# A pair's first product put into the bank of its sums by ScalarE and added to there by TensorE, in the feed-forward stage of an encoder block

## The chip, the cores and the metric

The kernel runs on one core of a Trainium2 chip, in one launch. The metric is the device time of one execution in microseconds. Of the kernel before, three runs were timed: 2977.9, 2979.1 and 2979.88 us, median 2979.1. One further execution was profiled. The engines are named as the profile names them: PE is TensorE (its matmuls), PEld its loads of weights, DVE is VectorE, ACT is ScalarE, POOL is GpSimd, SP is SyncE, which here issues the DMAs.

## The reference

One block of an encoder on 2048 tokens of width 1024: a mixing part (two groups of heads), a feed-forward part, and an embedding that is added through a gate. The change touches the feed-forward part alone:

```python
def conv_gated_mlp(xn, w_up, conv_w, conv_b, w_down):
    u = dwconv3_centred(xn @ w_up, conv_w, conv_b)
    gate, val = jnp.split(u, 2, axis=-1)
    return (jax.nn.silu(gate) * val) @ w_down
...
        h = h + conv_gated_mlp(rms_norm(h, ln_ffn_g[l]), w_up[l], conv_ffn_w[l],
                               conv_ffn_b[l], w_down[l])
```

`w_up` is 1024 x 5632, so gate and value have 2816 columns each; the convolution runs over three neighbouring tokens; `w_down` is 2816 x 1024.

## The kernel before, in words

**Products.** Everything is float32. A product is made as three products of split operands: a high part that TensorE takes fast (type fp32r) and a low part, the rest. `split` (L113) makes them: ScalarE casts the high part (L117), VectorE subtracts it from the source to get the low one (L120). `mm3` (L130 is its last line) issues low x high, high x low and high x high.

**Pairs.** `up_down` runs the two big products of the feed-forward part as a sequence of 68 pairs of 128-row tiles. Pairs 0 to 43 multiply by `w_up` (22 for the first half of the tokens, 22 for the second; each has one tile of gate and one of value columns), pairs 44 to 67 by `w_down` (three blocks of eight, each over a part of the 2816 rows). A pair is a 2 x 2 product of blocks, done in seven products in place of eight, after Strassen. The sums of the stationary operand (S1 to S4) and of the moving one (T1 to T4) are made ahead. Its seven products are A11 B11, S1 T1, S2 T2, A12 B21, S3 T3, A22 T4 and S4 B22. Each takes 12 matmuls of 128 x 512 (four depth steps of three), 9 in the last block.

**Banks.** A pair has two PSUM tiles of two banks: `fxy` with x and y, `fzs` with z and a spare bank, each tile in a ring of two. A11 B11 goes into x, and A12 B21 is added there. S1 T1 goes into z, and S4 B22 is added there. S2 T2 goes into y, and S3 T3 and A22 T4 are added there one after the other. Between two of them y is read out, since each partial sum is wanted by itself: after S2 and after S3 in the same pair, after A22 in the next. What all four results have in common, the first product A11 B11, is added outside: in the up pairs ScalarE copies x to a tile p1 (L1493), and VectorE adds p1 to y at each read; in the down pairs VectorE adds x into the output rows.

**After the products.** In up pairs the results lie in `ug` (gate) and `uv` (value), 1024 tokens and two of the neighbours each. `conv` (L1418) runs the three taps: an ACTIVATE on ScalarE, two scalar_tensor_tensor on VectorE for each of gate and value, Silu on ScalarE (L1434), a multiply, and a DMA to `hid_d`. In down pairs VectorE adds the results to rows of h (`fh`), which a DMA loaded, and another stores.

**Operands.** The moving operands of a block (seven names of four tiles) are loaded and split by `load_op` (L1280 is the DMA) when the block changes: at pairs 22, 44, 52 and 60. The loads of a name are issued where its old tiles have had their last use. `up_load` and `up_prep` fetch and split the stationary tiles of the pairs to come. `steps` spreads other sums over the pairs, `ple` the beginning of the last stage over the last block.

**Order.** The code is written pair by pair, but a scheduler puts the instructions of each engine in order; each engine then works strictly in its list, and semaphores hold it where an operand or a bank isn't ready. VectorE and ScalarE have one list each for reads of banks, splits of operands and the convolution, so a read of a bank can stand behind a split that waits for a DMA.

## Time and profile before

| what | value |
|---|---|
| timed runs | 2977.9, 2979.1, 2979.88 us |
| the profiled execution | 2982.03 us |
| its span | 2980.3 us |
| mean granted TensorE clock | 0.995 |
| TensorE matmul, busy | 2922.8 us, 98%, 14858 matmuls |
| VectorE, busy | 2065.7 us, 69% |
| ScalarE, busy | 1355.9 us, 45% |
| the stage `up_down` in the span | about 1436 to 2748 us |

Times in the views count from the start of the span. A row of the timeline has the start, the time taken, the engine, the line, the operation, output and inputs, and how many ran; in brackets is how long the engine stood idle before it and what released it. A row of waits has the engine that waited, the line waited for, the total, the number and the longest. Matmuls overlap each other (one lasts about 0.39 us, and the next starts 0.23 us after it), so a busy TensorE isn't yet one that goes at its full rate.

### The profile page before, as it was taken

To read this page: it belongs to the slowest core of one execution; us is meant where nothing else is said; L and a number is where in the kernel's file an instruction comes from. 1 tells how busy PE (TensorE), PEld (TensorE's weight loads), DVE (VectorE), ACT (ScalarE), POOL (GpSimd) and SP (SyncE) were. 2 spreads that over 40 slices of the span, in tenths; PEclk is the share of its full clock that TensorE was granted. 3 is DMA by queue.
4 is the path that set the end of the run, shared out by engine and by line. 5 is a ranking of instruction groups with operands and counts; after the bars stand their busy time and mean duration, and the time that the engine had idled before them with its cause. 6 is when DMAs were issued, how large, how long until landed. Compare 5 with 4: busy or idle time off the path is not lost. (4 is left out here: it accounts for less than half of the span.)

```text
span 2980.3 us, 40726 instructions
## 1 busy us (share of the span) xinstructions
PE 2922.8 (98%) x14858; PEld 2456.4 (82%) x14858; DVE 2065.7 (69%) x3799; ACT 1355.9 (45%) x2648; POOL 141.8 (5%) x262
## 2 busy tenths in 40 slices
PE   8999999999999999999999999999999999999999
PEld 7888888888889888788788887788887787877887
DVE  7522555677777777636688888778878777687665
ACT  6311544656656565523444445444445232233444
POOL 3100000000000000001000000000000000000111
PEclk9999999999999999999999999999999999999999
DMA  6512445343333343568544544557746656575221
GB/s 190 124 59 94 141 131 156 119 151 98 100 98 101 95 126 103 168 191 282 187 142 170 198 164 168 177 180 239 234 150 186 198 195 219 173 243 203 80 80 64
DMA packets 377401, 460.20 MB, mean 154 GB/s; under 512 B 30176, under 2 KB 263152, under 8 KB 377200
## 3 DMA queue, kind: packets, MB, share of 16 engines
q1 hardware_dynamic: 377200, 457.59, 47.9%
q8 instruction: 117, 1.92, 0.3%
q14 instruction: 84, 0.69, 0.1%
HBM read 294.26 MB, written 163.25 MB: 154 GB/s over the span
## 5 line engine op out<-in xcount | busy, mean ns | idle before, releaser
L130 PE MATMUL fxy<-op,fw 128*128 128x512 f32 x3168 | 757.9, 395 | 16.2 <-DVE fh L1387 11.6
L130 PEld LDWEIGHTS fxy<-op,fw 128*128 128x128 f32 x3168 | 590.4, 189 | 164.8 <-DVE fh L1387 21.9
L130 PE MATMUL fzs<-op,fw 128*128 128x512 f32 x1584 | 386.9, 390 | 1.1 <-DVE xt L1152 1.1
L130 PEld LDWEIGHTS fzs<-op,fw 128*128 128x128 f32 x1584 | 297.6, 188 | 63.5 <-DVE xt L1152 1.3
L130 PE MATMUL bk<-wsp,xh 128*128 128x512 f32 (+1 forms) x768 | 233.9, 386 | 0.0
L117 ACT CAST pt<-tb 128x512 fp32r<-128x512 f32 x256 | 147.1, 587 | 176.1 <-PE tb L977 175.5
L919 DVE TENSOR_REDUCE mx<-bk 128x1 f32<-128x512 f32 x256 | 175.2, 685 | 68.2 <-PE bk L918 63.7
L130 PE MATMUL ppv<-pt,kv 128*128 128x256 f32 x1536 | 203.9, 287 | 0.0
L120 DVE TENSOR_TENSOR pt<-tb,pt 128x512 fp32r<-128x512 f32 x256 | 174.2, 685 | 37.7 <-ACT pt L117 36.4
L130 PE MATMUL fxy<-op,fwd 128*128 128x512 f32 x792 | 192.0, 391 | 2.9 <-DVE c L1387 1.4
L937 ACT ACTIVATE pe<-bk,nm 128x512 f32<-128x512 f32 x256 | 174.6, 696 | 32.5 <-DVE nm L931 27.1
L130 PEld LDWEIGHTS ppv<-pt,kv 128*128 128x128 f32 x1536 | 189.0, 191 | 0.5 <-ACT pt L117 0.4
L130 PE MATMUL bk<-wo,yhl 128*128 128x512 f32 x744 | 176.1, 395 | 3.6 <-DVE yhl L120 3.6
L130 PE MATMUL pgp<-pw,x3s 128*128 128x512 f32 (+1 forms) x792 | 178.6, 384 | 0.0
L130 PEld LDWEIGHTS fxy<-op,fwd 128*128 128x128 f32 x792 | 147.8, 188 | 36.5 <-DVE uv L1387 3.3
L130 PEld LDWEIGHTS pgp<-pw,x3s 128*128 128x128 f32 x792 | 144.5, 188 | 28.3
L1387 DVE TENSOR_TENSOR fh<-fh,fxy 128x512 f32<-128x512 f32 (+1 forms) x139 | 104.9, 768 | 89.0 <-PE fxy L130 87.6
L130 PEld LDWEIGHTS bk<-wo,yhl 128*128 128x128 f32 x744 | 139.2, 189 | 32.5 <-DVE yhl L120 4.1
L130 PEld LDWEIGHTS bk<-wsp,xh 128*128 128x128 f32 x768 | 145.1, 189 | 25.0
L130 PE MATMUL bk<-wsp,xl 128*128 128x512 f32 (+1 forms) x384 | 150.5, 392 | 8.2 <-DVE xl L120 8.2
L117 ACT CAST fw<-hraw 128x1024 fp32r<-128x1024 f32 (+1 forms) x72 | 70.4, 980 | 191.8 <-PE fxy L130 116.1
L130 PE MATMUL bk<-xh,wqk 128*128 128x512 f32 x480 | 157.5, 393 | 0.0
(332 smaller groups left out, 5024.3 us busy)
## 6 DMA issues: line engine op xcount, KB each, us to landing
fwr<-in_w_up SPq DMA_DIRECT2D x66, 512.0 KB, 4.0
fh<-h_d SPq DMA_DIRECT2D x48, 512.0 KB, 5.0
h_d<-fh SPq DMA_DIRECT2D x48, 512.0 KB, 2.8
s_d<-fwr SPq DMA_DIRECT2D x44, 512.0 KB, 3.2
fws<-s_d SPq DMA_DIRECT2D x44, 512.0 KB, 3.6
rw<-row_d SPq DMA_DIRECT2D x32, 512.0 KB, 5.1
hraw<-hid_d SPq DMA_DIRECT2D x30, 512.0 KB, 4.5
tsum<-in_w_down SPq DMA_DIRECT2D x44, 256.0 KB, 4.2
```

The costliest lines, as they stand in the source:

```text
L117: nc.scalar.copy(hi, src)
L120: (sub or nc.vector).tensor_tensor(lo, src, _f(hi), op=ALU.subtract)
L130: mm = lambda *a, **k: self.nc.tensor.matmul(*a, **k, skip_group_check=more)
L919: nc.vector.tensor_reduce(s.mx[:, kb:kb + 1], ps, axis=AX.X, op=ALU.max)
L937: nc.scalar.activation(s.pe[:, kb % 2], s.banks[kb], AF.Exp, bias=s.nm, scale=ASCALE, accum_out=s.rs[:, kb:kb + 1])
L1387: add = lambda o, a, b: tt(o, a, b, op=ALU.add)
```

## The change

From pair 2 on (`seeded`), ScalarE copies the first product from bank x into bank y as soon as it is complete. S2, S3 and A22 are then all added to what is in the bank by TensorE (`more=True`, so that none of their matmuls starts the bank anew), and each read of y already holds the first product. With that

- VectorE's additions of p1 to y go: in up pairs the reads of y after S2 and after A22 become copies on ScalarE, and the read after S3 stays an addition on VectorE, but of z's first product (S1 T1, which ScalarE copies to a tile p5 when it is complete) in place of p1; the second addition to uv goes. In down pairs the addition of x to half a row and that of 128 x 1024 to a whole row go.
- `rest` is split: `rest_y` (A22, added to the previous pair's y) comes after S1 as before, `rest_z` (S4, added to the previous pair's z) after A12 of the pair. `conv` is split into its halves, the value's after `rest_y`, the gate's after `rest_z`.
- B22 of a new block is loaded after `rest_z`, and no longer together with T4 before S2. The steps of other sums move from after the rest to after the reads of S2 and of S3.
- within a product the twelve matmuls run as high x high for the four depth steps, then low x high, then high x low.

The number of matmuls stays. The diff without its repeats (`twice` and the old `rest`, `conv` and `prod` are in the listing above):

```diff
@@ prod
-            for k, (xh, xl) in enumerate(ops):
-                ks = slice(k * P, (k + 1) * P)
-                self.mm3(out, wh[:, ks], wl[:, ks], xh, xl, not more and k == 0, k == len(ops) - 1, more)
+            first, last = not more, len(ops) - 1
+            for a, lo in ((wh, 0), (wl, 0), (wh, 1)):
+                for k, parts in enumerate(ops):
+                    nc.tensor.matmul(out, a[:, k * P:(k + 1) * P], parts[lo], start=first,
+                                     stop=lo == 1 and k == last, skip_group_check=more)
+                    first = False
@@ rest, now rest_y and rest_z
+            elif s.seeded:
+                nc.scalar.copy(s.uv[:, 2:2 + SB], s.y)
             else:
                 add(s.uv[:, 2:2 + SB], s.p1, s.y)
+
+        def rest_z(s):
+
             prod(s.z, s.ops["S4"], "B22", True)
@@ the loop over pairs
+            s.seeded = i > 1
             prod(x, s.ops["A11"], "B11")
-            if i < NUP + 2:
-                s.p1 = s.spare if i > NUP else self.at(f"t{6 + i % 2}", [P, SB], name="p1")
+            if s.seeded:
+                nc.scalar.copy(s.y, x)
+            else:
+                s.p1 = self.at(f"t{6 + i}", [P, SB], name="p1")
                 nc.scalar.copy(s.p1, x)
             if s.down:
                 s.o = outs.pop(i)
-                p1 = s.p1 if i < NUP + 2 else x
-                add(s.o[0][:, H], s.o[0][:, H], p1)
-            if i > NUP:
-                add(twice(s.o[1]), twice(s.o[1]), p1.unsqueeze(1).broadcast_to([P, 2, SB]))
...
             prod(s.z, s.ops["S1"], "T1")
+            if s.seeded and not s.down:
+                s.p5 = self.at(f"t{6 + i % 2}", [P, SB], name="p5")
+                nc.scalar.copy(s.p5, s.z)
...
             if prev:
-                rest(prev)
-                if prev.i in steps:
-                    self.p1tag = f"t{6 + prev.i % 2}"
-                    next(steps[prev.i])
+                rest_y(prev)
+                if not prev.down:
+                    conv(prev, 1)
             if j == 0 and blk:
                 load(blk, "T4")
-                load(blk, "B22")
             side(2, 3, 4, 6)
-            prod(s.y, s.ops["S2"], "T2")
+            prod(s.y, s.ops["S2"], "T2", s.seeded)
             if s.down:
                 add(s.o[0][:, H], s.o[0][:, H], s.y)
             else:
                 s.ug = self.at(f"u{i % 2}", [P, 2 * SB + 2], name="ug")
-                add(s.ug[:, 2 + SB:2 + 2 * SB], s.p1, s.y)
+                if s.seeded:
+                    nc.scalar.copy(s.ug[:, 2 + SB:2 + 2 * SB], s.y)
+                else:
+                    add(s.ug[:, 2 + SB:2 + 2 * SB], s.p1, s.y)
+            if i in steps:
+                next(steps[i])
...
             side(7)
-            if prev and not prev.down:
-                conv(prev)
+            if prev:
+                rest_z(prev)
+                if not prev.down:
+                    conv(prev, 0)
+            if j == 0 and blk:
+                load(blk, "B22")
...
             prod(s.y, s.ops["S3"], "T3", True)
             if i == NUP:
                 c22 = self.at("t7", [P, SB], name="c22")
-                add(c22, s.p1, s.y)
+                nc.scalar.copy(c22, s.y)
                 add(c22, c22, s.z)
                 s.o += self.down_out(NUP, (1,))
-                add(s.o[1][:, L], s.o[1][:, L], s.p1)
...
             else:
                 s.uv = self.at("u2", [P, 2 * SB + 2], name="uv")
-                add(s.uv[:, 2 + SB:2 + 2 * SB], s.p1, s.y)
-                add(s.uv[:, 2 + SB:2 + 2 * SB], s.uv[:, 2 + SB:2 + 2 * SB], s.z)
+                add(s.uv[:, 2 + SB:2 + 2 * SB], s.p5 if s.seeded else s.p1, s.y)
+                if not s.seeded:
+                    add(s.uv[:, 2 + SB:2 + 2 * SB], s.uv[:, 2 + SB:2 + 2 * SB], s.z)
```

How that moves the instructions. The first place is TensorE in an up pair of the first half. Of the names, `fw` are split stationary tiles (A11 and A12 of a pair are the two halves of one, so they share a name; `op` are the moving operands), `fwd` is A22. Before, from the last matmuls of S2 (15246, 15247) through a part of the next pair's A11 (15366, 15367) to A12 (15231, 15232):

```order
L130 MATMUL fxy<-op,fw_15246 128x512 x2
L130 MATMUL fxy<-op,fw_15247 128x512
L130 MATMUL fxy<-op,fw_15246 128x512 x2
L130 MATMUL fxy<-op,fw_15367 128x512
L130 MATMUL fxy<-op,fw_15366 128x512 x2
L130 MATMUL fxy<-op,fw_15367 128x512
L130 MATMUL fxy<-op,fw_15366 128x512
L130 MATMUL fxy<-op,fw_15232 128x512
L130 MATMUL fxy<-op,fw_15231 128x512 x2
L130 MATMUL fxy<-op,fw_15232 128x512
L130 MATMUL fxy<-op,fw_15231 128x512 x2
```

After, one pair from S1 (15234) through A22 of the previous pair (`fwd`), S2 (15240, 15241), the first four of S4 of the previous pair (15106), A12 (15225, 15226), the other eight of S4, to S3 (15234):

```order
L1401 MATMUL fzs<-op,fw_15234 128x512 x12
L1401 MATMUL fxy<-op,fwd 128x512 x12
L1401 MATMUL fxy<-op,fw_15240 128x512 x4
L1401 MATMUL fxy<-op,fw_15241 128x512 x4
L1401 MATMUL fxy<-op,fw_15240 128x512 x4
L1401 MATMUL fzs<-op,fw_15106 128x512 x4
L1401 MATMUL fxy<-op,fw_15225 128x512 x4
L1401 MATMUL fxy<-op,fw_15226 128x512 x4
L1401 MATMUL fxy<-op,fw_15225 128x512 x4
L1401 MATMUL fzs<-op,fw_15106 128x512 x8
L1401 MATMUL fxy<-op,fw_15234 128x512 x12
```

Between S2 and A12, which both use the tile `fxy`, five matmuls of the next A11 stood before, and four of S4 stand now; between A12 and S3 stand eight of S4.

The second place is VectorE at the switch to the second block of down pairs (pair 52). `fh` are rows of h, and L1387 adds to them; `op` are the split operands. Before:

```order
L1387 TENSOR_TENSOR fh<-fh,fxy 128x512
L1387 TENSOR_TENSOR fh<-fh,fxy 128x1024
L1387 TENSOR_TENSOR fh<-fh,fxy 128x512
L120 TENSOR_TENSOR op<-opr,op 128x512 x2
L1387 TENSOR_TENSOR fh<-fh,fzs 128x512
L120 TENSOR_TENSOR op<-opr,op 128x512 x6
L1387 TENSOR_TENSOR fh<-fh,fxy 128x512
L120 TENSOR_TENSOR fw_22352<-hraw,fw_22351 128x1024
L120 TENSOR_TENSOR fwd<-hraw,fwd 128x512
```

After:

```order
L120 TENSOR_TENSOR op<-opr,op 128x512 x4
L1387 TENSOR_TENSOR fh<-fh,fxy 128x512
L120 TENSOR_TENSOR fwd<-hraw,fwd 128x512
L1368 TENSOR_TENSOR hraw<-hraw 128x512
L1369 TENSOR_TENSOR hraw<-hraw 128x512
L1375 TENSOR_TENSOR hraw<-hraw 128x512
L1376 TENSOR_TENSOR hraw<-hraw 128x512
L1387 TENSOR_TENSOR fh<-fh,fxy 128x512
L1387 TENSOR_TENSOR fh<-fh,fzs 128x512
L120 TENSOR_TENSOR fw_22322<-hraw,fw_22322 128x1024
L120 TENSOR_TENSOR fw_22317<-hraw,fw_22316 128x1024
L120 TENSOR_TENSOR op<-opr,op 128x512 x4
```

Of the last eight subtractions of the block's operands (T4 and B22), all stood ahead of the addition of S2's bank before (the seventh row, behind the runs of two and of six). After, a run of four stands ahead of it (the addition is the second row), and the other four stand behind the additions that follow.

The third place is ScalarE in a steady up pair of the second half, after the change. L1502 is the copy into the bank, L1442 Silu, L1515 the copy of z to p5, L1412 and L1533 the new reads of y, L1434 the ACTIVATE, L1553 the copy of A12's bank:

```order
L1502 COPY fxy<-fxy 128x512
L1442 ACTIVATE fgv<-fgv 128x1024
L1515 COPY p_19677<-fzs 128x512
L1412 COPY uv<-fxy 128x512
L117 CAST fwd<-fwr 128x512
L1434 ACTIVATE fgv<-uv,fcw 128x1024
L1533 COPY ug<-fxy 128x512
L117 CAST fw_19730<-fws 128x1024
L1553 COPY ug<-fxy 128x512
```

Between the read of y after A22 (L1412) and that after S2 (L1533) stand a cast of `fwd` and the value's ACTIVATE; of these copies only that of A12's bank stood in ScalarE's list before, and the one of the first product to p1.

More of the change, by code (lines that the diff above doesn't have):

```diff
@@ L1388, in up_down @@
         L, H = slice(0, SB), slice(SB, 2 * SB)
-        twice = lambda t: t.rearrange("p (a t) -> p a t", a=2)
         NUP, blocks = self.NUP, self.BLOCKS
@@ L1398, in prod, with rest_y @@
             ops = self.xop[x]
-            for k, (xh, xl) in enumerate(ops):
-                ks = slice(k * P, (k + 1) * P)
-                self.mm3(out, wh[:, ks], wl[:, ks], xh, xl, not more and k == 0, k == len(ops) - 1, more)
-        def rest(s):
+            first, last = not more, len(ops) - 1
[4 more added lines that the diff above has]
+                    first = False
+        def rest_y(s):
             prod(s.y, s.ops["A22"], "T4", True)
@@ L1416, in rest, with conv @@
                 add(s.ug[:, 2 + SB:2 + 2 * SB], s.ug[:, 2 + SB:2 + 2 * SB], s.z)
-        def conv(s):
+        def conv(s, half):
             b, c = divmod(s.i, NC2)
-            ts = []
-            for half, u in enumerate((s.ug, s.uv)):
-                ct = half * NC2 + c
-                if b:
-                    nc.vector.tensor_copy(u[:, 0:2], edge[:, ct])
-                else:
-                    nc.vector.memset(u[:, 0:2], 0.0)
-                t = self.at(("w7", "w11")[half], [P, 2 * SB], name="fgv")
-                nc.scalar.activation(t, u[:, 0:2 * SB], AF.Identity, bias=taps[:, 3, ct:ct + 1], scale=taps[:, 0, ct:ct + 1])
-                for tap in (1, 2):
-                    nc.vector.scalar_tensor_tensor(t, u[:, tap:tap + 2 * SB], taps[:, tap, ct:ct + 1], t,
-                                                   op0=ALU.mult, op1=ALU.add)
-                nc.scalar.copy(edge[:, ct], u[:, 2 * SB:2 * SB + 2])
-                if half == 0:
-                    nc.scalar.activation(t, t, AF.Silu)
-                ts.append(t)
-            tt(ts[0], ts[1], ts[0], op=ALU.mult)
+            u = s.uv if half else s.ug
+            ct = half * NC2 + c
             if b:
-                nc.sync.dma_start(self.hid_d[c, :, 2 * SB - 1:4 * SB - 1], ts[0])
+                nc.vector.tensor_copy(u[:, 0:2], edge[:, ct])
             else:
-                nc.sync.dma_start(self.hid_d[c, :, 0:2 * SB - 1], ts[0][:, 1:])
+                nc.vector.memset(u[:, 0:2], 0.0)
+            t = self.at(("w7", "w11")[half], [P, 2 * SB], name="fgv")
+            nc.scalar.activation(t, u[:, 0:2 * SB], AF.Identity, bias=taps[:, 3, ct:ct + 1], scale=taps[:, 0, ct:ct + 1])
+            for tap in (1, 2):
+                nc.vector.scalar_tensor_tensor(t, u[:, tap:tap + 2 * SB], taps[:, tap, ct:ct + 1], t,
+                                               op0=ALU.mult, op1=ALU.add)
+            nc.scalar.copy(edge[:, ct], u[:, 2 * SB:2 * SB + 2])
+            if half:
+                s.val = t
+                return
+            nc.scalar.activation(t, t, AF.Silu)
+            tt(t, s.val, t, op=ALU.mult)
+            if b:
+                nc.sync.dma_start(self.hid_d[c, :, 2 * SB - 1:4 * SB - 1], t)
+            else:
+                nc.sync.dma_start(self.hid_d[c, :, 0:2 * SB - 1], t[:, 1:])
             if s.i < NUP - 1:
@@ L1522, in up_down @@
                 s.ug = self.at(f"u{i % 2}", [P, 2 * SB + 2], name="ug")
-                add(s.ug[:, 2 + SB:2 + 2 * SB], s.p1, s.y)
+                if s.seeded:
+                    nc.scalar.copy(s.ug[:, 2 + SB:2 + 2 * SB], s.y)
+                else:
+                    add(s.ug[:, 2 + SB:2 + 2 * SB], s.p1, s.y)
+            if i in steps:
+                next(steps[i])
             if i == 1:
@@ L1560, in up_down @@
                 s.uv = self.at("u2", [P, 2 * SB + 2], name="uv")
-                add(s.uv[:, 2 + SB:2 + 2 * SB], s.p1, s.y)
-                add(s.uv[:, 2 + SB:2 + 2 * SB], s.uv[:, 2 + SB:2 + 2 * SB], s.z)
+                add(s.uv[:, 2 + SB:2 + 2 * SB], s.p5 if s.seeded else s.p1, s.y)
+                if not s.seeded:
+                    add(s.uv[:, 2 + SB:2 + 2 * SB], s.uv[:, 2 + SB:2 + 2 * SB], s.z)
+                if i in steps:
+                    self.p1tag = f"t{6 + i % 2}"
+                    next(steps[i])
             if i == 0:
@@ L1567, in up_down @@
             load(then, "T3")
-            if i in steps:
-                next(steps[i])
             prev = s
         next(ple)
-        rest(prev)
+        rest_y(prev)
+        rest_z(prev)
         for _ in ple:
```

## The prediction

> **What bounds the kernel now.** I read the page first. One engine is busy for nearly the whole span:
>
> ```profile
> span 2980.3 us, 40726 instructions
> PE 2922.8 (98%) x14858; PEld 2456.4 (82%) x14858; DVE 2065.7 (69%) x3799; ACT 1355.9 (45%) x2648; POOL 141.8 (5%) x262
> ```
>
> TensorE sets the time, and the change leaves it the same number of matmuls. So only two things can move: the moments in which TensorE stands, and the clock that it is granted. The second view is the table of windows over the stage that changes. Its columns are the stretch, its length, then busy time and count of TensorE, weight loads, VectorE, ScalarE and GpSimd, then granted TensorE clock, DMA share and GB/s. I cut it where blocks of operands change (pairs 21 to 22, 43 to 44, 51 to 52).
>
> ```profile
> 1436.00:1496.00 60.00, 58.34 (x258) 46.31 (x257) 45.48 (x59) 31.53 (x45) 0.74 (x2) 1.00 0.58 187
> 1496.00:1846.00 350.00, 350.00 (x1530) 284.07 (x1530) 298.63 (x385) 157.98 (x208) 0.00 (x0) 1.00 0.48 164
> 1846.00:1896.00 50.00, 44.88 (x187) 35.13 (x186) 42.66 (x60) 27.81 (x44) 0.00 (x0) 0.97 0.78 249
> 1896.00:2278.00 382.00, 382.00 (x1674) 311.89 (x1673) 303.09 (x371) 174.81 (x228) 0.00 (x0) 1.00 0.58 188
> 2278.00:2345.00 67.00, 57.70 (x232) 45.91 (x231) 58.76 (x84) 30.72 (x45) 0.00 (x0) 0.92 0.72 225
> 2345.00:2465.00 120.00, 120.00 (x527) 97.92 (x526) 86.68 (x118) 34.92 (x46) 0.00 (x0) 1.00 0.58 193
> 2465.00:2480.00 15.00, 12.73 (x50) 10.08 (x48) 13.41 (x20) 4.95 (x8) 0.00 (x0) 0.89 0.88 297
> 2480.00:2655.00 175.00, 174.78 (x763) 141.72 (x762) 130.97 (x186) 49.76 (x69) 0.00 (x0) 1.00 0.61 203
> 2655.00:2748.00 93.00, 91.35 (x399) 72.16 (x398) 69.02 (x99) 28.71 (x40) 3.30 (x8) 1.00 0.61 213
> ```
>
> The three long quiet stretches (350, 382, 120) take 852 us for 3731 matmuls, 0.2284 us each. At that rate the first switch loses 50 - 187 x 0.2284 = 7.3 us, the second 67 - 232 x 0.2284 = 14.0, the third 15 - 50 x 0.2284 = 3.6. That is 24.9 us in 132 us. The other edges together lose about 3.7 (60 - 258 x 0.2284 = 1.1, 0.7 and 1.9). So the stage is bound by TensorE, except at three places. Third view, the waits of TensorE's matmuls and of its weight loads in 1436 to 2748 (total, times, longest):
>
> ```profile
> PE fxy L130 <- DVE fh L1387: 11.9, 7, 4.2
> PE fxy L130 <- DVE fw L120: 3.1, 1, 3.1
> PE fxy L130 <- DVE c L1387: 1.4, 1, 1.4
> PEld fxy L130 <- DVE ug L1387: 8.6, 29, 1.4
> PEld fxy L130 <- ACT ug L1539: 8.1, 36, 0.3
> ```
>
> Nearly all matmul waits are for VectorE, at the switches. The timeline there shows what VectorE was held by. First switch:
>
> ```profile
> 1873.18 1.30 ACT L117 CAST op<-opr 128x512 fp32r<-128x512 f32 x2 [1.91 <-DMA opr<-t_d]
> 1875.64 1.22 DVE L120 TENSOR_TENSOR fw<-fwr,fw 128x1024 fp32r<-128x1024 f32 x1
> 1876.91 5.33 PE L130 MATMUL fxy<-op,fw 128*128 128x512 f32 x14 [3.12 <-DVE fw L120]
> ```
>
> Second switch, from up to down:
>
> ```profile
> 2303.92 2.00 DVE L120 TENSOR_TENSOR op<-opr,op 128x512 fp32r<-128x512 f32 x3
> 2305.84 0.68 DVE L1387 TENSOR_TENSOR fh<-fh,fxy 128x512 f32<-128x512 f32 x1
> 2306.57 10.99 PE L130 MATMUL fxy<-op,fw 128*128 128x512 f32 x36 [4.21 <-DVE fh L1387]
> ...
> 2318.95 1.40 PE L130 MATMUL fxy<-op,fwd 128*128 128x512 f32 x5 [1.39 <-DVE c L1387]
> ...
> 2329.15 0.69 DVE L1387 TENSOR_TENSOR fh<-fh,p 128x512 f32<-128x512 f32 x1 [1.56 <-DMA fh<-h_d]
> 2331.09 3.98 PE L130 MATMUL fxy<-op,fw 128*128 128x512 f32 x11 [3.69 <-DVE fh L1387]
> ```
>
> Third switch:
>
> ```profile
> 2467.27 2.88 PE L130 MATMUL fxy<-op,fw 128*128 128x512 f32 x12
> ...
> 2468.07 3.70 DVE L120 TENSOR_TENSOR op<-opr,op 128x512 fp32r<-128x512 f32 x6
> 2471.68 0.68 DVE L1387 TENSOR_TENSOR fh<-fh,fxy 128x512 f32<-128x512 f32 x1
> ...
> 2472.42 2.93 PE L130 MATMUL fxy<-op,fw 128*128 128x512 f32 x6 [2.27 <-DVE fh L1387]
> ```
>
> The pattern is the same each time. A short add that frees a PSUM bank stands in VectorE's queue behind several subtractions of operands (L120), and these stand behind casts that wait for a DMA. TensorE has the next product for that bank close behind, so it stops. After the stall it is slow as well: 12 matmuls took 2.88 us before it, six took 2.93 after it. The clock column prices that at most at 50 x 0.03 + 67 x 0.08 + 15 x 0.11 = 8.5 us of the 24.9.
>
> **The change part by part.** The durations on which it rests (tile fxy over the whole stage as minimum/median/maximum ns, then groups of 1500 to 1846 with their mean ns):
>
> ```profile
> L1387 DVE TENSOR_TENSOR ug<-p,fxy x44: 679/682/686, 1448.9 to 2283.2; 128x512 f32<-128x512 f32 x44
> L1539 ACT COPY ug<-fxy x44: 574/580/592, 1453.7 to 2287.1; 128x512 f32<-128x512 f32 x44
> L1493 ACT COPY fzs<-fxy x1: 575/575/575, 2318.2 to 2318.2; 128x512 f32<-128x512 f32 x1
> L120 DVE TENSOR_TENSOR op<-opr,op 128x512 fp32r<-128x512 f32 x5 | 3.3, 687 | 0.0
> L1428 ACT ACTIVATE fgv<-uv,fcw 128x1024 f32<-128x1024 f32 x18 | 22.4, 1246 | 1.8
> L1434 ACT ACTIVATE fgv<-fgv 128x1024 f32<-128x1024 f32 x18 | 19.1, 1063 | 8.8 <-DVE fgv L1430 7.4
> L117 ACT CAST fwd<-fwr 128x512 fp32r<-128x512 f32 x18 | 11.2, 624 | 43.7 <-PE fxy L130 37.1 <-DMA hid_d<-fgv 6.6
> ```
>
> *Seed copy.* For pairs 2 to 67 ScalarE copies the first product into the other bank of the tile, 0.575 us by the one PSUM to PSUM copy there is. In the up pairs it takes the place of the copy to p1, so it is free there. In the down pairs it is new. S2 needs it, and 24 matmuls (S1 and the previous A22) lie between, 24 x 0.2265 = 5.4 us. Here 0.2265 is the free rate, (2.88 - 0.39)/11 from the row of 12. Cost: nothing, unless ScalarE is late by 4 us.
>
> *Adds removed.* An up pair loses three VectorE adds (ug, uv, and the second add of uv): 3 x 0.68 = 2.0 us off 298.63/350 x 19.2 = 16.4 us of VectorE per pair. ScalarE gains three copies, 3 x 0.58 = 1.7 us, on 157.98/350 x 19.2 = 8.7. A down pair loses a 512 and a 1024 wide add. None of this is on TensorE's path while VectorE keeps up, so by itself it is worth nothing in the quiet stretches.
>
> *Steady up pairs.* Before, TensorE waits twice in a pair: A12 for VectorE's add of S2 with five matmuls of cover, and S3 for ScalarE's copy with four. Together they cost at most (350/1530 - 0.2265) x 84 = 0.19 us per pair. After, A12 waits for ScalarE's copy of S2 with four matmuls, and S3 for ScalarE's copy of A12 with eight. One wait of the ScalarE kind is left, so about half: gain 0.09 x 40 = 3.6 us at most. The condition is that ScalarE is free when S2 ends. Since A22 ended, one product ago, it has to do the uv copy, the fwd cast and an ACTIVATE: 0.58 + 0.62 + 1.25 = 2.45 us, against 12 x 0.2265 = 2.72. The slack is 0.27 us. I take a gain of 2. Steady down pairs keep VectorE's add of S2 ahead of A12, now with four matmuls where it had about as many: nothing, at worst 0.1 x 24 = 2.4 us lost.
>
> *Order of the partial products in prod.* Same count, same tiles, only another order within twelve matmuls: nothing. It needs the low halves four matmuls later, which can only help.
>
> *Third switch.* B22 is now loaded after the rest of the previous pair. In the order, four subtractions that stood ahead of the add move behind it, 4 x 0.687 = 2.7 us, more than the wait of 2.27. The wait goes and the slow clock with it; next late is the steady wait. I leave 0.3: gain 3.3. If the four that remain still wait for their DMA, 1 to 2 us stay.
>
> *Second switch.* A12 of pair 44 now has S4 of pair 43 and A11 of pair 45 ahead of it, 24 matmuls or 5.4 us, against a wait of 4.21: it goes. The c22 wait (1.39) becomes ScalarE's copy, 0.1 us shorter and otherwise the same. The last (3.69) is half a queue, half a DMA (1.56): the add of p that waited for it is removed, but the next add to that tile waits for the same load. I keep 1.4 + 3.7 + 1.4 of slow clock, 6.5 of 14.0: gain 7.5, between 4 (only the first stall goes) and 12.
>
> *First switch.* ScalarE's new copies of S2 stand behind the same casts as VectorE's subtractions did, and such a cast waited 1.91 us. I expect the 3.12 and its slow clock (up to 1.5) to go, and about 1 us to come back at ScalarE in pairs 21 and 22: 3.5 of 7.3 left, gain 3.8, between 0 and 6.
>
> *SP's queue.* The B22 loads, four per switch, move behind the first half of the rest. They are needed an iteration later by S4, so nothing waits.
>
> The sum: 3.8 + 7.5 + 3.3 + 2 = 16.6, less 1.6 for ScalarE copies that come late at the block ends (one 1.91 us DMA wait, roughly): 15 us. The profiled execution took 2982.03 us, 1.73 over its span, and would come to 2967. The median of the timed runs is 2979.1, 2.9 below that execution, so I forecast 2979.1 - 15 = 2964.1.
>
> **A rule weighed.** Row first: at the third switch a wait of 2.27 us was followed by six matmuls in 2.93 us, with a granted clock of 0.89 in that window, while the 1.39 us wait at 2318.95 is not followed by such a stretch (five matmuls in 1.40 us). So here something between 1.4 and 2.3 us of standing is enough to be slowed down. The Trainium skill, page "TensorE: Matmul & The Clock Gate", Part 1, puts the change to half clock after an idle window of about 3.4 us. By that rule a remaining stall of 2.3 to 3.4 us would cost only itself, and the sum would be up to 1.4 us better at the second switch; the trace disagrees, and I go by the trace.
>
> **The rivals.**
> *No change.* The stalls at the switches begin with a DMA (1.91 us for t_d, 1.56 for h_d), and the loads are the same. If ScalarE's copies merely take VectorE's place behind the same casts, the first two switches keep their 21 us and only the third and the steady pairs gain, 3.3 + 2 = 5, or 2974. For it: DMA share 0.72 to 0.88 at the switches against 0.48 to 0.61 elsewhere. Against it: the 4.21 and 2.27 us waits end with VectorE's queue, not with a landing.
> *Slower.* ScalarE becomes the late one in every up pair. The place is the copy of S2, on which A12 now hangs with four matmuls of cover and 0.27 us of slack. ScalarE works in its order, and Silu (L1434), which waits for VectorE's taps, stands a few places ahead of that copy. Were Silu so late that its 1.06 us fell into the product before, each pair would lose 1.06 - 0.27 = 0.8 us: 40 x 0.8 = 32, less 16.6, +15 us, 2994. It decides from a lateness of (16.6 + 6)/40 + 0.27 = 0.84 us per pair. Against it: ScalarE is busy only 45% there, and 54% after.
> *Much faster.* All three switches close, clock included: 24.9 + 3.6, 2951.
> *That the seed is not added to* would change the values, not the time, so it is no case of its own.
>
> **How the numbers follow.** Forecast (gain 7 to 24 us) 0.62; no change (within 6 us) 0.17; slower 0.13; much faster 0.08. A difference of 0.2%, 6 us, is about what a measurement of this kernel can tell from none. Faster is 0.62 + 0.08 = 0.70, same 0.17, slower 0.13. The range takes in the gains of all switches at their best (2950) and the no-change case with 2 us lost (2981); the slower case and the far end of the fastest are left out, under 2 in 10.
>
> **What would show it.** Right: the clock in the windows of the second and third switch at 0.97 or more; no wait of TensorE for L120; the wait for VectorE's ug add gone, with about 40 short ones for ScalarE's copy of S2 in its place; VectorE about 2 us lighter per up pair. Wrong: ScalarE waits over 0.5 us in each quiet pair, or the switches still lose 20 us with ScalarE or a DMA as the releaser.

## The result, and the profile after

The changed kernel takes 2962.49 us (median of 4 runs, 2958.88 to 2964.82) against 2979.49 us of the kernel before (4 runs). The ratio is 0.9941, 95% interval 0.9923 to 0.9958: faster by 17.0 us, 0.6%. The forecast was a gain of 15 us, to 2964.1.

The page of the profiled execution (2958.88 us):

```profile
span 2957.1 us, 40739 instructions
PE 2911.9 (98%) x14858; PEld 2453.5 (83%) x14858; DVE 1956.8 (66%) x3624; ACT 1434.4 (49%) x2797; POOL 141.9 (5%) x262
```

Matmuls are the same in number. The same stretches of the stage, with their edges moved by the time gained so far (columns as in the prediction):

```profile
1492.00:1842.00 350.00, 350.00 (x1541) 287.49 (x1540) 268.57 (x330) 186.70 (x261) 0.00 (x0) 1.00 0.47 162
1842.00:1885.00 43.00, 41.32 (x180) 33.13 (x179) 38.05 (x53) 32.51 (x53) 0.00 (x0) 1.00 0.86 281
1885.00:2266.00 381.00, 381.00 (x1667) 309.37 (x1666) 266.79 (x306) 203.21 (x283) 0.00 (x0) 1.00 0.58 185
2266.00:2323.00 57.00, 53.06 (x224) 42.76 (x223) 53.20 (x77) 34.18 (x52) 0.00 (x0) 0.97 0.74 242
2323.00:2443.00 120.00, 120.00 (x526) 98.06 (x525) 77.93 (x107) 38.47 (x52) 0.00 (x0) 1.00 0.63 206
2443.00:2454.50 11.50, 11.50 (x52) 9.38 (x52) 9.73 (x15) 3.52 (x6) 0.00 (x0) 1.00 0.96 321
```

At the switches TensorE now stands little, and at the third not at all. The clock is 1.00 at the first and third and 0.97 at the second (0.97, 0.92 and 0.89 before). The waits of the whole stage:

```profile
PE fxy L1401 <- DVE fh L1387: 4.5, 4, 2.2
PE fxy L1401 <- ACT ug L1533: 2.5, 2, 1.6
PEld fxy L1401 <- ACT ug L1533: 11.5, 42, 2.0
```

No wait for L120 is left, and the waits for VectorE's ug add are two short ones; in their place stand 42 of the weight queue for ScalarE's read of S2, one in nearly every up pair, 0.27 us on average. VectorE is 109 us lighter, ScalarE 79 us heavier.

To compare kernels stretch by stretch I count the 5544 matmuls of the stage in each trace and cut at the same counts (those that fall on the edges of the prediction's windows in the trace of before). The table gives microseconds of one profiled execution for each kernel, the experiments below among them; "up" and "down" are the quiet stretches. (The trace of the changed kernel with B22 early lacks three of these matmuls, so its cuts can lie 0.7 us off.)

| kernel | start | up 1 | switch 1 | up 2 | switch 2 | down 1 | switch 3 | down 2 | end | stage |
|---|---|---|---|---|---|---|---|---|---|---|
| before | 57.7 | 350.1 | 50.0 | 381.8 | 67.0 | 120.2 | 15.0 | 175.0 | 88.8 | 1305.7 |
| changed | 57.8 | 347.8 | 44.5 | 382.7 | 58.8 | 120.3 | 10.9 | 175.5 | 87.5 | 1285.9 |
| seed alone | 57.5 | 351.8 | 45.2 | 382.6 | 55.2 | 120.4 | 10.9 | 177.2 | 86.7 | 1287.5 |
| order alone | 57.0 | 350.0 | 47.9 | 386.3 | 68.5 | 125.2 | 12.4 | 185.1 | 90.0 | 1322.5 |
| order alone, S4 early in down pairs | 57.3 | 349.9 | 48.4 | 386.2 | 67.7 | 120.2 | 14.8 | 176.1 | 91.0 | 1311.7 |
| before, B22 late | 57.9 | 350.1 | 45.7 | 381.7 | 67.9 | 120.2 | 11.6 | 176.7 | 88.5 | 1300.4 |
| changed, B22 early | 57.2 | 348.0 | 44.6 | 382.7 | 62.8 | 120.2 | 11.4 | 175.9 | 87.4 | 1290.2 |
| changed, reads on VectorE | 58.1 | 350.3 | 48.3 | 386.4 | 60.6 | 120.3 | 10.9 | 177.8 | 88.0 | 1300.6 |
| changed, VectorE's load back | 57.2 | 349.1 | 45.3 | 383.8 | 62.2 | 125.6 | 12.1 | 185.9 | 92.5 | 1313.9 |
| changed, uv copied three times | 57.9 | 354.6 | 44.0 | 387.8 | 58.2 | 120.3 | 10.9 | 178.5 | 87.2 | 1299.5 |
| changed, old order in a product | 57.9 | 347.8 | 45.2 | 382.6 | 56.1 | 120.3 | 11.5 | 181.8 | 89.0 | 1292.1 |
| late preparation | 58.5 | 347.8 | 45.6 | 380.5 | 56.6 | 120.3 | 10.9 | 177.6 | 87.2 | 1285.0 |
| late preparation, old order at switch 2 | 57.0 | 347.8 | 44.1 | 380.5 | 65.5 | 120.3 | 10.9 | 178.4 | 88.8 | 1293.3 |
| late preparation, low halves on GpSimd | 57.7 | 347.9 | 53.6 | 380.5 | 70.9 | 124.1 | 13.3 | 182.3 | 87.7 | 1318.1 |

The stage got 19.8 us shorter: 5.5 + 8.2 + 4.1 = 17.8 at the switches, 2.3 in the first quiet stretch, 1.3 at the end; the second quiet stretch lost 0.9. The two profiled executions differ by 23.2 us. The rest, 3.3 us, lies ahead of the stage, where the program is the same; some of it is the clock, which in 520 to 532 us was granted at 0.72 in the one and 0.86 in the other (12 x 0.14 = 1.7 us).

```profile
520.00:532.00 12.00, 8.48 (x36) 6.73 (x34) 8.57 (x18) 10.24 (x17) 0.00 (x0) 0.72 0.41 131
```

```profile
520.00:532.00 12.00, 8.70 (x44) 7.32 (x44) 8.29 (x17) 11.08 (x17) 0.00 (x0) 0.86 0.39 128
```

(the kernel before, then the changed one). Differences between runs of one kernel are of that size.

The slow clock has a part in the gain at the switches too. By the clock column it cost at most 8.5 us there before (the prediction's sum) and at most 57 x 0.03 = 1.7 us after; so up to 6.8 of the 17.8 us are slow clock that no longer follows a stall. The last section shows that it doesn't follow every stall.

### The profile page after: what moved, and what is told of

It is laid out like the page before. It is cut to its first block, busy times and chain, and to the rows that moved or that the text cites. A ratio compares the mean times of both kernels' runs of the same rounds, so it can differ in the third digit from the quotient of the medians.

```text
span 2957.1 us, 40739 instructions
## 1 busy us (share of the span) xinstructions
PE 2911.9 (98%) x14858; PEld 2453.5 (83%) x14858; DVE 1956.8 (66%) x3624; ACT 1434.4 (49%) x2797; POOL 141.9 (5%) x262
## 3 DMA queue, kind: packets, MB, share of 16 engines
q1 hardware_dynamic: 377200, 457.59, 48.3%
## 5 line engine op out<-in xcount | busy, mean ns | idle before, releaser
L919 DVE TENSOR_REDUCE mx<-bk 128x1 f32<-128x512 f32 x256 | 175.0, 685 | 69.0 <-PE bk L918 64.3
L120 DVE TENSOR_TENSOR pt<-tb,pt 128x512 fp32r<-128x512 f32 x256 | 174.0, 685 | 37.2 <-ACT pt L117 35.8
L130 PE MATMUL pgp<-pw,x3s 128*128 128x512 f32 (+1 forms) x792 | 178.5, 384 | 0.0
L977 PE MATMUL tb<-ident,pe 128*128 128x128 f32 x1024 | 149.9, 273 | 3.2 <-DVE pt L120 3.2
L977 PEld LDWEIGHTS tb<-ident,pe 128*128 128x128 f32 x1024 | 121.9, 140 | 21.8 <-DVE pt L120 4.6
```

The source lines that it names most:

```text
L120: (sub or nc.vector).tensor_tensor(lo, src, _f(hi), op=ALU.subtract)
L130: mm = lambda *a, **k: self.nc.tensor.matmul(*a, **k, skip_group_check=more)
L919: nc.vector.tensor_reduce(s.mx[:, kb:kb + 1], ps, axis=AX.X, op=ALU.max)
L977: nc.tensor.transpose(t[:, j, :], s.p[kb][:, j * P:(j + 1) * P], self.ident)
```

## The experiments

The theory after the result: the switches gained because reads of banks left VectorE's queue, where they stood behind subtractions of operands, and because other products were put between. Rivals: the relief of VectorE alone, the order alone, the late B22 alone. The experiments were run in three batches, each beside new runs of the kernel before (medians 2979.09, 2979.60 and 2981.51 us), and each ratio is to those of its batch. So totals of different batches, the changed kernel's 2962.49 among them, can be compared to some 2 us only.

**Seed alone.** The seeds, the reads by ScalarE and p5 as in the change; all that concerns order as before:

```diff
             if prev:
-                rest_y(prev)
-                if not prev.down:
-                    conv(prev, 1)
+                rest_y(prev)
+                rest_z(prev)
...
                 load(blk, "T4")
+                load(blk, "B22")
```

> The first product is put into the bank and added to there, and ScalarE reads the bank, as in the changed kernel; but A22 and S4 of the pair before stay together ahead of S2, the convolution stays whole, B22 is loaded with T4, and the products run low x high first, as before. What stands between S2 and A12 is then four matmuls of the next pair's A11. Theory (the reads of the banks left VectorE's queue AND other products were put between; each closes a part of the stalls): about half of the 17 us, 2968 to 2975. Rival 1 (the relief of VectorE alone does it, the order is idle): 2960 to 2965. Rival 2 (the order alone does it): 2977 to 2983.

Measured: 2967.32 us, ratio 0.9956 (0.9943 to 0.9970), just under the theory's range. The table says more than the total: the three switches take 45.2, 55.2 and 10.9, 20.7 less than before and 2.9 less than in the changed kernel. So no other product between any two is needed there. The new order gives its part elsewhere: with the seed alone the first quiet stretch takes 351.8 (350.1 in the kernel before) and 347.8 in the changed kernel. With the seed alone A12 waits there for a read with four matmuls of cover, and S3 for another with four.

**Order alone.** The changed kernel without a seed (and with the steps of other sums where they stood before):

```diff
-            s.seeded = i > 1
+            s.seeded = False
...
+                p1 = s.p1 if i < NUP + 2 else x
+                add(s.o[0][:, H], s.o[0][:, H], p1)
+            if i > NUP:
+                add(twice(s.o[1]), twice(s.o[1]), p1.unsqueeze(1).broadcast_to([P, 2, SB]))
```

> The split rest and convolution, the late B22 and the new order within a product, but no seed: VectorE adds the first product at each read, as in the kernel before. Theory (both parts do it): 2966 to 2974. Rival 1 (the relief of VectorE alone): 2976 to 2983. Rival 2 (the order alone): 2960 to 2965.

Measured: 2999.02 us, ratio 1.0061 (1.0048 to 1.0073). All three were wrong: it is slower than the kernel before. Most of the loss is in the down pairs, 5.0 and 10.1 us in the two quiet stretches; another 4.5 us are lost in the second quiet up stretch (386.3 against 381.8). The timeline of one of the down pairs, and the row of VectorE's waits for rows of h in 2347 to 2670:

```profile
2352.20 1.82 DVE L1387 TENSOR_TENSOR fh<-fh,fxy 128x1024 f32<-128x1024 f32 x2 [5.11 <-DMA fh<-h_d]
2353.47 2.83 PE L1401 MATMUL fxy<-op,fw 128*128 128x512 f32 x11 [1.67 <-DVE fh L1387]
```

```profile
DVE fh L1387 <- DMA fh<-h_d: 47.2, 14, 5.5
```

In the kernel before this wait is, in 2345 to 2655:

```profile
DVE fh L1387 <- DMA fh<-h_d: 1.2, 1, 1.2
```

VectorE adds the first product to the rows right after A11, and TensorE can't go on in that bank until it has. The rows now land later than they did. The next run tested whether the late place of S4 is the reason.

**Order alone, with S4 right after A22 in the down pairs** (and, with it, B22 of the blocks from pair 52 on loaded with T4 again):

```diff
                 if not prev.down:
                     conv(prev, 1)
+                if i > NUP:
+                    rest_z(prev)
```

> As the run with the order alone (no seed), but in the down pairs S4 of the pair before comes right after A22 again. Theory (without a seed VectorE adds the first product to the rows right after A11; with S4 late the rows of the pair before are stored late, the tiles come free late and the next rows land late, so that this add waits for its DMA and holds the bank): the down stretches go back to 120 and 175 us, the waits of VectorE for rows from 47 us to under 3, 2976 to 2984 in all. Rival (VectorE's load in the new order is what costs): 2992 to 3000.

Measured: 2986.17 us, ratio 1.0017 (1.0008 to 1.0026). The down stretches are back at 120.2 and 176.1, and the wait for rows is this, in 2340 to 2665:

```profile
DVE fh L1387 <- DMA fh<-h_d: 1.8, 1, 1.8
```

So the place of S4 is the cause there: it is what finishes a row, and only a row that is stored gives its tile to the next. In total the run is 2 us above the theory's range: without the seed the switches and the end stay slow (48.4, 67.7, 14.8 with B22 early again, 91.0), and the second quiet up stretch does not go back. It takes 386.2 to 386.4 us in this run, the one before and the run "reads on VectorE" below. In all three VectorE reads the bank of S2 with four matmuls of cover; there the weight loads wait 6.5 or 6.6 us in all for that read, and 3.7 us for ScalarE's in the changed kernel.

**VectorE's load back.** The changed kernel, with a maximum of the same data with itself where an add is gone (no value changes):

```diff
+            keep = lambda t: tt(t, t, t, op=ALU.max)
             if s.down:
                 s.o = outs.pop(i)
+                keep(s.o[0][:, H])
+            if i > NUP:
+                keep(s.o[1])
```

(and likewise behind the three places in the up pairs).

> The changed kernel with VectorE's load put back: where an add of the first product is gone, VectorE takes the maximum of the same row half (or of the 128 x 1024 row) with itself, which changes no value; no PSUM bank hangs on it. Theory (the stalls at the switches closed because VectorE's queue is about 2 us per pair shorter): 8 to 16 us of the gain go again, most of them in the three switch windows, 2970 to 2979. Rival (they closed because the banks are no longer read through VectorE's queue): 2960 to 2966.

Measured: 2992.07 us, ratio 1.0043 (1.0030 to 1.0056), 13 us over the upper end of the theory. But not where the theory had it. The first switch stays at 45.3, the second goes from 58.8 to 62.2, and the quiet up stretches lose 1.3 and 1.1. So 2 us more of VectorE per up pair (three instructions of 0.69) cost almost nothing. The loss is in the down pairs again (125.6, 185.9, 92.5), with the same cause, in 2340 to 2665:

```profile
DVE fh L1507 <- DMA fh<-h_d: 55.3, 18, 6.3
```

An instruction that touches the rows early holds VectorE's whole queue until they land, even if no bank hangs on it. The seed takes these early instructions out of the down pairs; with them the new order is a loss.

**Reads on VectorE.** The seed and the order as changed, two reads back on VectorE:

```diff
-                nc.scalar.copy(s.uv[:, 2:2 + SB], s.y)
+                nc.vector.tensor_copy(s.uv[:, 2:2 + SB], s.y)
...
-                    nc.scalar.copy(s.ug[:, 2 + SB:2 + 2 * SB], s.y)
+                    nc.vector.tensor_copy(s.ug[:, 2 + SB:2 + 2 * SB], s.y)
```

> The changed kernel, with the two new reads of y in the up pairs (after A22 to uv, after S2 to ug) made by VectorE and not by ScalarE; seed and p5 copies stay on ScalarE. Theory (a read on VectorE lasts 0.68 us and not 0.58 with four matmuls of cover, 0.1 x 42 = 4 us, and at the first two switches it stands behind the subtractions again, 2 to 6 us): 2966 to 2973. Rival (it doesn't matter which engine reads, the adds that are gone and the order do it): 2960 to 2965.

Measured: 2972.63 us, ratio 0.9976 (0.9966 to 0.9986), in the theory's range. The first switch gives back 3.8 of its 5.5 us, the second 1.8, the quiet up stretches lose 2.5 and 3.7 (6.2, where 4 were expected). At the first switch both reads stand behind a run of subtractions again:

```profile
1846.04 3.69 DVE L120 TENSOR_TENSOR op<-opr,op 128x512 fp32r<-128x512 f32 x6
1849.65 0.68 DVE L1412 COPY uv<-fxy 128x512 f32<-128x512 f32 x1
1850.86 0.69 DVE L1533 COPY ug<-fxy 128x512 f32<-128x512 f32 x1
```

But this isn't what TensorE's matmuls stood for. These are the waits that the view gives for them in 1835 to 1895, and both are for ScalarE:

```profile
PE fzs L1401 <- ACT op L117: 2.0, 2, 1.0
PE fxy L1401 <- ACT ug L1553: 1.3, 1, 1.3
```

The granted clock is 0.89 in 1870 to 1885, another 1.6 us. So the run shows that the place of the reads matters at this switch, not that the reads themselves were what TensorE waited for; how they delay ScalarE's casts stays open. In the quiet stretches the cause is the one named above, the wait for the read of S2.

**ScalarE's slack.** The copy of y to uv made three times:

```diff
-                nc.scalar.copy(s.uv[:, 2:2 + SB], s.y)
+                for _ in range(3):
+                    nc.scalar.copy(s.uv[:, 2:2 + SB], s.y)
```

> The changed kernel, with ScalarE's copy of y to uv (ahead of the read on which A12 hangs) made three times in each up pair: the same values, two more ScalarE copies of about 0.5 us each in its queue. In the trace of the changed kernel ScalarE stood 0.42 us before the read of S2 in a steady pair. Theory (that 0.42 us is the whole slack, and what exceeds it is lost by TensorE one for one): (2 x 0.5 - 0.42) x 42 pairs = 24 us more than the changed kernel's 2962, 2980 to 2992. Rival 1 (no slack, all of it counts): 42 us more, 3000 to 3008. Rival 2 (TensorE has other products to do, nothing counts): 2960 to 2966.

Measured: 2973.88 us, ratio 0.9981 (0.9972 to 0.9990), 11.4 us over the changed kernel and not 24. ScalarE in a steady pair of the changed kernel, and here:

```profile
1651.38 0.59 ACT L1412 COPY uv<-fxy 128x512 f32<-128x512 f32 x1 [2.18 <-PE fxy L1401]
...
1654.05 0.59 ACT L1533 COPY ug<-fxy 128x512 f32<-128x512 f32 x1 [0.42 <-PE fxy L1401]
```

```profile
1657.28 0.59 ACT L1413 COPY uv<-fxy 128x512 f32<-128x512 f32 x1 [2.19 <-PE fxy L1401]
...
1660.68 0.57 ACT L1534 COPY ug<-fxy 128x512 f32<-128x512 f32 x1
```

The read of S2 comes 3.40 us after that of A22 instead of 2.67, 0.73 late. The first quiet stretch lost 6.8 us in about 18 pairs, 0.37 each. The order shows why it isn't more: in this kernel the scheduler put six matmuls of S4 between S2 and A12 in the steady up pairs, and not four, 2 x 0.2265 = 0.45 us more cover. 0.73 - 0.45 = 0.28, and in the trace the two steps from matmul to matmul at A12 grew by 0.26 us (from 0.23 + 0.27 to 0.42 + 0.34). The rest, about 0.1, is a cast that moved ahead of the copy of A12, as below. What exceeds slack and cover is lost one for one; but the cover is no constant, since the scheduler weighs it anew.

**B22, from both sides.** First the changed kernel with B22 loaded early:

```diff
                 load(blk, "T4")
+                load(blk, "B22")
...
-            if j == 0 and blk:
-                load(blk, "B22")
```

> The changed kernel with one thing undone: B22 of a new block is loaded together with T4, ahead of S2, as in the kernel before. Theory of the prediction (the four subtractions of B22 that stood ahead of VectorE's add of S2 are what the third switch lost): the third switch loses 2 to 4 us again, and the others something, 2965 to 2970. Rival (the stall closed because two adds, 1.9 us, are gone from VectorE in each down pair; the run in which the seed came alone, with B22 loaded early, lost nothing there): the third switch stays closed, 2960 to 2965.

Measured: 2967.60 us, ratio 0.9961 (0.9948 to 0.9973). It doesn't answer the question cleanly. With S4 of the old block's last pair still to come, this edit makes that product multiply by the new block's B22 in place of the old one's, so this kernel computes something else, and the product also waits for that load: at the second switch TensorE waits 4.4 us, before a product into z's tile, for the cast of an operand. That switch takes 62.8 us, which brings the total into the theory's range; the third takes 11.4 and stays closed, as the rival had it. The edit does show that the late load belongs to the late S4. The clean test is the other side, the kernel before with B22 late:

```diff
                 load(blk, "T4")
-                load(blk, "B22")
...
             if prev and not prev.down:
                 conv(prev)
+            if j == 0 and blk:
+                load(blk, "B22")
```

> The kernel before with one edit: B22 of a new block is loaded after A12, behind the rest of the pair before, and not with T4. Theory of the prediction (four subtractions fewer ahead of VectorE's add of S2 close the third switch): the third switch takes 11.7 us and not 15.0, 2973 to 2977 in all. Rival (the stall there needs the adds to go from VectorE's queue, or the reads): the third switch keeps 14 to 15 us, 2977 to 2982.

Measured: 2976.50 us, ratio 0.9983 (0.9975 to 0.9992), in the range of the theory. The third switch takes 11.6 us, as worked out, and the first 45.7, 4.3 less; the second stays (67.9). VectorE's add of S2 at the third switch now stands behind two subtractions, not six:

```profile
2463.98 1.29 DVE L120 TENSOR_TENSOR op<-opr,op 128x512 fp32r<-128x512 f32 x2
...
2466.32 0.68 DVE L1387 TENSOR_TENSOR fh<-fh,fxy 128x512 f32<-128x512 f32 x1
2466.45 8.51 PE L130 MATMUL fxy<-op,fw 128*128 128x512 f32 x36 [0.40 <-DVE fw L120]
```

At the first switch the longest wait, the one for L120, is still there:

```profile
1875.23 5.78 PE L130 MATMUL fxy<-op,fw 128*128 128x512 f32 x24 [2.58 <-DVE fw L120]
```

It was 3.12 us in the kernel before, and 14 matmuls then took 5.33 us; here 24 take 5.78. So some 2 of the 4.3 us are the slow clock, which didn't follow this time.

**The order within a product**, as it was:

```diff
-            for a, lo in ((wh, 0), (wl, 0), (wh, 1)):
+            for k, (xh, xl) in enumerate(ops):
+                self.mm3(out, wh[:, ks], wl[:, ks], xh, xl, not more and k == 0, k == len(ops) - 1, more)
```

> The changed kernel with the matmuls of a product in the old order again: for each depth step low x high, high x low, high x high. Theory (the order within a product is idle): 2960 to 2965, each stretch within 0.5 us of the changed kernel's. Rival (needing the low halves four matmuls later spares waits at the switches): 2 to 5 us more, 2965 to 2968, all of it in the switch windows.

Measured: 2966.10 us, ratio 0.9949 (0.9936 to 0.9961), in the rival's range. It is 3.6 us over the changed kernel by the medians and 2.4 by the ratios, whose intervals overlap. And it isn't for the rival's reason. The quiet up stretches and the first down stretch are equal to 0.1 us. The excess is one stall at the start of the last block, in "down 2" (181.8 against 175.5). There VectorE's read of a bank stood behind a subtraction, this behind a cast on ScalarE, and this waited for a weight of the kernel's last stage:

```profile
2602.82 0.62 ACT L117 CAST pw<-pwr 128x512 fp32r<-128x512 f32 x1 [4.99 <-DMA pwr<-in_w_ple_proj]
2603.47 0.69 DVE L120 TENSOR_TENSOR pw<-pwr,pw 128x512 fp32r<-128x512 f32 x1 [4.49 <-ACT pw L117]
...
2604.08 0.68 DVE L1387 TENSOR_TENSOR fh<-fh,fxy 128x512 f32<-128x512 f32 x1
...
2604.82 2.50 PE L130 MATMUL fxy<-op,fw 128*128 128x512 f32 x5 [4.36 <-DVE fh L1387]
```

In the quiet stretches the order within the products is idle. Whether the order moves that load was not tried; "down 2" also takes 177.2 to 178.5 in five other runs with the seed, so part of that difference need not be the order's.

**Late preparation.** In the second half of the up pairs the changed kernel puts a cast ahead of the copy of A12, on which S3 waits. First the changed kernel, then the run with `up_prep` and `up_load` written behind that copy:

```diff
-            if i + 1 < n:
-                self.up_prep(i + 1)
-            if i + 2 < n:
-                self.up_load(i + 2)
...
                 nc.scalar.copy(s.ug[:, 2:2 + SB], x)
+            if i + 1 < n:
+                self.up_prep(i + 1)
+            if i + 2 < n:
+                self.up_load(i + 2)
```

```profile
2081.72 1.05 ACT L117 CAST fw<-fws 128x1024 fp32r<-128x1024 f32 x1 [3.10 <-PE fxy L1401]
2082.68 0.58 ACT L1553 COPY ug<-fxy 128x512 f32<-128x512 f32 x1
```

```profile
2085.34 0.59 ACT L1549 COPY ug<-fxy 128x512 f32<-128x512 f32 x1 [3.10 <-PE fxy L1401]
2085.82 1.05 ACT L117 CAST fw<-fws 128x1024 fp32r<-128x1024 f32 x1
```

> The changed kernel with the preparation of the next pair's operands written behind ScalarE's copy of A12 and not ahead of it, so that in the second half of the up pairs the cast of 1.05 us comes after that copy. In the changed kernel each of those pairs stood 82 ns longer at S3 behind it, the pairs of the first half did not. Theory: that gap goes, 20 x 0.08 = 1.6 us, 2959 to 2963, and the quiet stretch of the second half gets shorter by 1.6 us in the trace. Rival (the casts come later, and another product waits for them): 2962 to 2968.

Measured: 2959.71 us, ratio 0.9931 (0.9917 to 0.9945). The second quiet stretch takes 380.5, 2.2 less than the changed kernel's 382.7 (1.6 expected). The total is the best of all, but its interval overlaps that of the change.

**The old order at the second switch**, on top of that:

```diff
+                if i in (NUP, NUP + 1):
+                    rest_z(prev)
             if j == 0 and blk:
                 load(blk, "T4")
+                if i in (NUP, NUP + 1):
+                    load(blk, "B22")
```

> As the run with the late preparation, and at the switch from up to down (pairs 44 and 45) S4 of the pair before comes right after A22 again, and B22 of that block is loaded early, as in the run with the seed alone, which lost 55.2 us there against 58.8 of the changed kernel. Theory (at that switch the old order is the better one, since S4's late read holds back the stores and loads of rows): 3 us less than the late preparation alone, 2956 to 2961. Rival (that difference came with the run's other order): 2959 to 2966.

Measured: 2965.56 us, ratio 0.9953 (0.9941 to 0.9966). The theory fell: the second switch takes 65.5, not 55, and the total is in the rival's range. What made it 55.2 with the seed alone stays open. About 1.7 of the 3.6 us between that run and the changed kernel are slow clock (1.00 with the seed alone, 0.97 in the changed kernel), and the late preparation takes 56.6 with the new order as it is.

**Low halves on GpSimd:**

```diff
-            self.split(raw, hi, lo)
+            self.split(raw, hi, lo, sub=self.nc.gpsimd if blk else None)
```

> As the run with the late preparation, and the low halves of a new block's operands (from the second block on) are made by GpSimd, which is idle there, and not by VectorE. Theory (what is left of the stalls at the second switch, about 5 us, is VectorE's add of rows behind these subtractions): 2 to 4 us less, 2955 to 2958. Rival 1 (the stalls are set by the loads themselves, the queue behind them doesn't matter): 2958 to 2962. Rival 2 (GpSimd takes more than twice VectorE's 0.69 us for one, and products wait for the low halves): 2965 to 2985.

Measured: 2993.60 us, ratio 1.0042 (1.0030 to 1.0055), worse than even the second rival had it. One subtraction takes 1.7 us there and not 0.69:

```profile
L120 POOL TENSOR_TENSOR op<-opr,op 128x512 fp32r<-128x512 f32 x105 | 176.5, 1717 | 1027.8 <-ACT op L117 1027.8
```

All switches get longer (53.6, 70.9, 13.3). The second rival had products wait for the low halves, but TensorE's matmuls never waited for GpSimd. The DMA issues did: a load into a tile isn't issued before the subtraction that reads the tile is done. In 1830 to 1900 the issues of operand loads (L1280) waited as follows, here and in the run with the late preparation:

```profile
SPq L1280 <- POOL op L120: 28.4, 21, 1.9
```

```profile
SPq L1280 <- DVE op L120: 12.6, 17, 3.2
```

The queue was moved, and its instructions got longer.

## Why the prediction was right, point by point

*The total* was right: -17.0 against -15. That the two are so near is in part luck, as the points on the first two switches show. *What bounds the kernel* was right: 17.8 of the 19.8 us in the trace came from 132 us at the three switches.

*Third switch* (3.3 forecast, 4.1 found). The step was that the four subtractions of B22 move behind the add. Tried alone, it does that: 15.0 to 11.6. But the seed alone, with B22 early, closes it as well (10.9). Either is enough, so the gain is not to be counted for both.

*Second switch* (7.5 forecast, 8.2 found). Here the step failed, though the size was right. It gave the gain to the 24 matmuls that the new order puts ahead of A12. With the order alone the switch takes 68.5 us, as long as before; with the seed alone 55.2. The gain is the seed's. The parts of the sum changed places as well. The prediction let the first stall (4.21 us) go and kept the last (3.69) and the wait for c22 (1.39). In the trace of the change the last two are gone, and the first is still there with 2.22 us and its slow clock, although the 24 matmuls do stand ahead of it (the two rows of 12):

```profile
2290.37 2.88 PE L1401 MATMUL fzs<-op,fw 128*128 128x512 f32 x12
...
2293.09 2.88 PE L1401 MATMUL fxy<-op,fw 128*128 128x512 f32 x12
...
2294.24 3.29 ACT L117 CAST op<-opr 128x512 fp32r<-128x512 f32 x5 [1.23 <-DMA opr<-tw_d]
...
2297.43 0.58 ACT L1502 COPY fxy<-fxy 128x512 f32<-128x512 f32 x1
2297.45 0.68 DVE L1387 TENSOR_TENSOR fh<-fh,fxy 128x512 f32<-128x512 f32 x1
...
2298.19 4.61 PE L1401 MATMUL fxy<-op,fw 128*128 128x512 f32 x12 [2.22 <-DVE fh L1387]
```

VectorE's read of the bank stands behind subtractions, and these behind casts that wait for a DMA. The cover only let TensorE arrive earlier; the load landed no sooner. So 8.2 beside 7.5 is luck. The seed copy itself (L1502) also stands behind the casts, which the prediction had priced at nothing. It ended 0.1 us before the read that released TensorE, so here it cost nothing more.

*First switch* (3.8 forecast, 5.5 found). "The pattern is the same each time" was not right here: the 3.12 us wait was not for an add that frees a bank, but for the subtraction that makes a stationary tile (`fw`). The 3.12 us wait for L120 and the slow clock went, and 1.57 us came back at ScalarE, where about 1 was said:

```profile
1843.67 0.62 ACT L117 CAST op<-opr 128x512 fp32r<-128x512 f32 x1 [2.01 <-DMA opr<-t_d]
...
1847.37 0.58 ACT L1533 COPY ug<-fxy 128x512 f32<-128x512 f32 x1
...
1848.00 3.01 PE L1401 MATMUL fxy<-op,fw 128*128 128x512 f32 x12 [1.57 <-ACT ug L1533]
```

What closes it is not settled. With the reads on VectorE 3.8 us come back, but as waits for ScalarE and slow clock. The late B22 takes 4.3 us off the kernel before, but leaves the wait for L120 at 2.58; and in the new order the switch takes 47.9 to 48.4 without the seed and 48.3 with the reads on VectorE, though B22 is late there. In every run with the seed and ScalarE's reads but that with the low halves on GpSimd it takes 44.0 to 45.6, with B22 early or late.

*Steady up pairs* (gain 2 forecast). Net 2.3 - 0.9 = 1.4. In the first half it was 0.13 us per pair, a little over the 0.09 worked out; in the second half a loss. The step said that S3 has eight matmuls of cover and so waits for nothing. It had missed that a cast of the next pair stands ahead of that copy in the second half, 1.05 us, though the listing of ScalarE's order shows it; taking it away gave 2.2 us.

*ScalarE's slack* (0.27) was 0.42 in the trace. The rival that hung on it was priced right in kind: lateness beyond slack and cover counted nearly one for one when it was added.

*The adds removed, "by itself worth nothing in the quiet stretches".* Right for the up pairs (putting their load back cost 1.2 us a stretch). For the down pairs the sentence was right only beside the old order. In the new one the early adds to rows would have cost 15 us in the two quiet stretches, and more at the end.

*The 1.6 us for late ScalarE copies at block ends*: matmuls did wait 2.5 us for ScalarE's read of S2, 1.57 of it at the first switch, but these lie within the gains of the switches given above; beside them no such loss is seen. The 2.4 feared in steady down pairs were not found (120.3 against 120.2, 175.5 against 175.0).

*The rule weighed.* The trace of the change has one stretch of slow clock in the stage, after a wait of 2.2 us. This is below the idle window of about 3.4 us that the Trainium skill gives on the page "TensorE: Matmul & The Clock Gate", Part 1, as was the wait at the third switch before; the measurement decides, and the prediction was right to go by it.

## What to carry to other kernels

Where TensorE is at 98%, look at the places where blocks change: the short read that frees a bank should not stand in a queue behind conversions that wait for a DMA, and any one of several edits may be enough (at the third switch a later load or fewer instructions), so their gains don't add up. An order that makes a result later also makes its store, its buffer and the next load later; it is safe only if nothing at the head of a queue touches that load early. Price a wait by what stands ahead of it in its engine's list, and by the load that this waits for, not by the cover alone.

## What the runs showed of the hardware

The slow clock does not follow from the length of a wait alone. In the run with the low halves on GpSimd a wait of 1.79 us (at 1856.8) was followed by it and one of 2.04 us (at 2282.6) was not:

```profile
1848.00:1862.00 14.00, 10.53 (x39) 7.94 (x38) 11.07 (x8) 10.47 (x17) 14.00 (x9) 0.88 0.73 215
2280.00:2290.00 10.00, 6.87 (x29) 5.08 (x28) 9.47 (x6) 6.05 (x10) 10.00 (x7) 1.00 0.76 218
```

```profile
1856.82 5.50 PE L1401 MATMUL fxy<-op,fw 128*128 128x512 f32 x16 [1.79 <-ACT ug L1549]
```

```profile
2282.65 3.02 PE L1401 MATMUL fxy<-op,fw 128*128 128x512 f32 x12 [2.04 <-ACT ug L1533]
```

Behind the first wait 16 matmuls took 5.50 us, where 15 x 0.2265 + 0.39 = 3.8 would do: 1.7 more. Behind the second the 12 took 3.02, near the usual 2.88. The wait of 2.58 us in the kernel before with B22 late was not followed by it either. The Trainium skill, page "TensorE: Matmul & The Clock Gate", Part 1, says that the window by which the clock is set runs freely and isn't started by the work. The waits agree with that. So a stall of about 2 us cost itself here, or 1.7 us more. A stretch of two traces may then differ by that much without a cause in the kernel; how often was not counted.
